# A two-layer hybrid decoder trunk: another order of TensorE's work at the block boundaries

## The chip, the cores and the metric

The kernel runs on one core of a Trainium2 chip. The metric is device time in microseconds (us) for one execution; one execution is also taken by the hardware profiler, and its span and its rows are quoted here. TensorE (PE in the profile) multiplies and transposes, VectorE (DVE) and ScalarE (ACT) do the elementwise work, GpSimd (POOL) takes square roots of reciprocals as powers and starts the DMAs that add onto a tile, and SyncE (SP) starts the plain loads.

## The reference

Each of two layers updates 512 tokens of 1024 features three times. With `h = rmsnorm(x)`:

```python
x = x + 0.5 * swiglu(rmsnorm(x, ffn1_norm), w1, w3, w2)     # d_ff 2816
p = rmsnorm(x, mix_norm) @ w_in                             # 8 pieces of 256 columns
mix = concat([conformer_conv(...), short_gated_conv(...), multiscale_pool(...), chunked_spatial_gating(...)])
x = x + mix @ w_out
x = x + 0.5 * swiglu(rmsnorm(x, ffn2_norm), w1, w3, w2)
```

After the second layer one more rmsnorm gives the output. All values are float32.

## The kernel before

**Tokens and numbers.** The 512 tokens stand in four blocks `b` of 128 rows; the "later" tokens are blocks 2 and 3 (half `r = 1`), the earlier ones blocks 0 and 1 (half `r = 0`). The residual stream lies in SBUF as `xt[b]`, token rows by features. Every float32 matrix is split into a high part (rounded to the matmul type by ScalarE) and a low part (the rest, subtracted by VectorE), and each product is three matmuls, high by high, weight-high by low (or the reverse), and low by high: `mm3`, whose three matmuls are lines 107, 108 and 109 of the profile. So every matrix on either side costs a cast on ScalarE and a subtraction on VectorE before all its three matmuls can run.

**A boundary.** At the end of a block (feed-forward or mixers) the result of each token block is added to `xt[b]` by VectorE. `Norm.square` (line 136, ScalarE) sums the squares of half a row, and `Norm.scale` (line 141) adds them up (`nv`, line 147), takes the power on POOL (`ry`, line 114) and makes the normed rows `xn` on VectorE (line 150), in one of two buffers. `Norm.turn(b)` (line 169) turns `xn` with 8 transposes on TensorE (line 157) and splits the result into high (line 204 or 183, ScalarE) and low parts (line 205 or 184, VectorE). The next block's matmuls read those splits: `B12` and `B22` for the later tokens, `B11` and `B21` for the earlier ones in a feed-forward, `h` and `l` in the mixers. The feed-forwards use one level of a Strassen-like scheme over halves of the tokens, and so also sums of these operands (`T1` to `T4`, `third` and `split`).

**Names.** `f0a`, `f0b`, `f1a`, `f1b` are the four feed-forwards in order, `L0` and `L1` the mixers of the two layers: f0a, L0, f0b, f1a, L1, f1b. Norm `n` feeds f0a, `m` feeds the mixers, `b` feeds f0b and f1b, and `a` feeds f1a.

**The start of a feed-forward (`up`).** It begins with the odd last slice of the hidden units: 4 weight tiles `w[m, k]` (two for each half `m` of that slice) are cast and split (`whi`, line 272; `wlo`, line 274), then for `r` = 1 and 0, for `m`, for `e` (w1 or w3) and for eight steps `k`, `mm3` follows. That is 96 matmuls of 256 columns for each `r`. Between the two `r` stand `third()` and `turns()`, the 16 transposes of the earlier token blocks. After it the ten other slices go through seven products each; slice 0 has two DMAs on POOL that add one weight tile onto another (lines 327 and 330), each after the plain load of the tile underneath.

**The end of the mixers.** `part(b, c)` (line 749) is 18 matmuls of 512 columns for one token block and one half of the features. After the last of these parts, an ending of 6 matmuls for each `b` and `c` adds the conformer's share, in the order `b` = 2, 3, 0, 1; then both blocks of the later tokens are turned. The weights of the endings (`wa`) lie in four tiles at `q0` to `q3`; `q2` and `q3` are also the home of `B22` and `B12`. The three `whi` and `wlo` buffers are shared: the next feed-forward's first splits take those that the last `part` has read.

**The start of the mixers.** `values(1)`, then the gate and the value projection of the later tokens, `turns()`, then both projections of the earlier tokens.

**What sets the order.** TensorE's instructions go out as they stand in the program (`tc.manual_schedule` at the bottom), and it works them off in that order. In `down`, VectorE and ScalarE also have the written order. Everywhere else a scheduler at build time orders each engine's queue by priority and by when it thinks the operands are there; `tc.high_priority` lifts the boundary's steps. Each engine then works its queue in order.

Of the kernel before, what the change touches and what calls it, by code (L numbers as in the profile page):

```python
# [10 lines left out]
F32 = mybir.dt.float32  # L11
F32R = mybir.dt.float32r
AF = mybir.ActivationFunctionType
ALU = mybir.AluOpType

P = 128
T = 512
D = 1024
KD = D // P
# [30 lines left out]
def trunk(ctx: ExitStack, tc: tile.TileContext, x, par, gains, tab, w13, w2, wi, wg, wo, out):  # L50
    nc = tc.nc
    V, S, G, PE = nc.vector, nc.scalar, nc.gpsimd, nc.tensor

    const = ctx.enter_context(tc.tile_pool(name="const", bufs=1))
    acts = ctx.enter_context(tc.tile_pool(name="acts", bufs=1))
# [15 lines left out]
    xt = [acts.tile([P, D], F32, name=f"x{b}", tag=f"x{b}") for b in range(NB)]  # L71
# [13 lines left out]
    def bank(name, shape=(P, T)):  # L85
        return psm.tile(list(shape), F32, tag="ps", name=name)


    def load(src, shape, name):
        raw = wts.tile(list(shape), F32, tag="raw", name=f"raw_{name}", bufs=6)  # L90
        nc.sync.dma_start(raw, src)
        return raw

    def split_w(raw, shape, name, pool=None, tags=("whi", "wlo")):
        pool = pool or wts
        hi = pool.tile(list(shape), F32R, tag=tags[0], name=f"whi_{name}")
        S.copy(hi, raw)  # L97
        lo = pool.tile(list(shape), F32R, tag=tags[1], name=f"wlo_{name}")
        V.tensor_tensor(lo, raw, hi.bitcast(F32), ALU.subtract)
        return hi, lo  # L100
# [4 lines left out]
    def mm3(ps, sh, sl, mh, ml, first, last, more=False):  # L105

        PE.matmul(ps, sh, mh, start=first, stop=False, skip_group_check=more)  # L107
        PE.matmul(ps, sh, ml, start=False, stop=False, skip_group_check=more)  # L108
        PE.matmul(ps, sl, mh, start=False, stop=last, skip_group_check=more)  # L109
# [128 lines left out]
    HALF = (slice(0, 256), slice(256, 512))  # L238
# [3 lines left out]
    def up(f, nrm, turns, name):  # L242
# [18 lines left out]
        def quarters(i):  # L261
            return {
                (m, k): load(w13[f, i, m, k], W, f"{name}{i}{m}{k}") for m in range(2) for k in range(2)
            }
# [3 lines left out]
        raw = quarters(i)  # L268
        w = {}
        for n, (m, k) in enumerate(((0, 0), (0, 1), (1, 0), (1, 1))):  # L270
            hi = wts.tile(list(W), F32R, tag="whi" if n < 3 else "raw", name=f"whi_{name}{i}{m}{k}", bufs=3 if n < 3 else 6)
            S.copy(hi, raw[m, k])
            lo = wts.tile(list(W), F32R, tag="wlo" if n < 3 else "raw", name=f"wlo_{name}{i}{m}{k}", bufs=3 if n < 3 else 6)
            V.tensor_tensor(lo, raw[m, k], hi.bitcast(F32), ALU.subtract)
            w[m, k] = hi, lo
        ps = {(m, e): bank(f"p{2 * e + 1}_{name}{i}{m}") for m in range(2) for e in range(2)}
        for r in (1, 0):
            for m in range(2):
                for e in range(2):
                    for k in range(KD):  # L280
                        hi, lo = w[m, k // 4]
                        g = nrm.op[f"B{k // 4 + 1}{r + 1}"]
                        mm3(
                            ps[m, e][:, HALF[r]], hi[:, e, k % 4], lo[:, e, k % 4],
                            g[0][:, k % 4], g[1][:, k % 4], k == 0, k == KD - 1,
                        )
            if r == 1:
                nrm.third()
                turns()
        for m in range(2):  # L290
            sg = tmp.tile([P, T], F32, tag="sg", name=f"sg_{name}{i}{m}", bufs=1)
            S.activation(sg, ps[m, 0], AF.Silu)
# [23 lines left out]
        for i in range(KH - 1):  # L316
            j, jj = i // 2, i % 2
            to = {(m, r): a[m][j][:, jj, HALF[r]] for m in range(2) for r in range(2)}
            nm = f"{name}{i}"
# [215 lines left out]
    def ffn(f, nrm, nxt, name, turns, end=False):  # L535
        down(f, *up(f, nrm, turns, name), nxt, name, end)
# [23 lines left out]
    def mixers(l, nrm, nxt, turns):  # L560
        base = l * C_LAYER
        nm = f"L{l}"
        scratch = Scratch(nm)

        def col(c):
            return pt[:, c : c + 1]
# [14 lines left out]
        def proj_mm(p, w, c=slice(0, T)):  # L581
            for k in range(KD):
                ks = slice(k * P, (k + 1) * P)
                mm3(p[:, c], w[0][:, ks], w[1][:, ks], nrm.h(k)[:, c], nrm.l(k)[:, c], k == 0, k == KD - 1)
# [9 lines left out]
        for i, home in enumerate(((acts, ("a04", "a14")), (None, ("whi", "wlo")))):  # L594
            raw = load(wg[l, :, i * D : (i + 1) * D], (P, D), f"{nm}g{i}")
# [42 lines left out]
        wgate, wval = proj_w(2), proj_w(0)  # L638
        pg, pv = bank(f"pi_{nm}2"), bank(f"pi_{nm}0")
        proj_mm(pg, wgate, HALF[1])  # L640
        proj_mm(pv, wval, HALF[1])
        turns()
        proj_mm(pg, wgate, HALF[0])
        proj_mm(pv, wval, HALF[0])
        gated(0, pg, pv)
# [4 lines left out]
        mix = {}  # L650
# [90 lines left out]
        wr, pw = {}, {}  # L741
# [7 lines left out]
        def part(b, c):  # L749
            pw[b, c] = bank(f"po_{nm}{b}{c}")  # L750
            bs = slice(b * P, (b + 1) * P)
            for i in range(3):
                for e in range(2):
                    hi, lo = mix[MIX_ORDER[2 * i + e]]
                    mm3(
                        pw[b, c], hi[:, bs], lo[:, bs], wr[c, i][0][:, e], wr[c, i][1][:, e],
                        i == 0 and e == 0, False,
                    )
# [25 lines left out]
        for b in range(NB):  # L784
            for j in range(2):
                PE.matmul(
                    pst[:, b : b + 1], ya[j][0][:, b * P : (b + 1) * P], ones[:, 0:1],
                    start=(j == 0), stop=(j == 1),
# [10 lines left out]
        for j in range(2):  # L799
            y, sg = ya[j][1], ya[j][0]  # L800
            g, b = col(base + C_CG + j), col(base + C_CBB + j)
# [4 lines left out]
            mix[j] = split2(y, f"ya_{nm}{j}")  # L806


        wa = []
        for c in range(2):  # L810
            raw = load(wo[l, c, :, 6:8], (P, 2, T), f"{nm}oa{c}")
            wa.append(split_w(raw, (P, 2, T), f"{nm}oa{c}", acts, (f"q{2 * c}", f"q{2 * c + 1}")))
        part(0, 1)
        part(1, 1)
        for b in (2, 3, 0, 1):
            bs = slice(b * P, (b + 1) * P)
            for c in range(2):
                for e in range(2):
                    hi, lo = mix[e]
                    mm3(pw[b, c], hi[:, bs], lo[:, bs], wa[c][0][:, e], wa[c][1][:, e], False, e == 1)  # L820
                with tc.high_priority(offset=400):
                    xs = xt[b][:, c * T : (c + 1) * T]
                    V.tensor_tensor(xs, pw[b, c], xs, ALU.add)
                nxt.square(b, c)
            nxt.scale(b)
        for b in (2, 3):
            nxt.turn(b)


    ctx.enter_context(tc.manual_schedule(engines={mybir.EngineType.PE}))  # L830
# [4 lines left out]
    nrm = Norm("n0", 0)  # L835
# [14 lines left out]
    for l in range(DEPTH):  # L850

        def turns(nrm=nrm):
            for b in (0, 1):
                nrm.turn(b)

        nx = Norm(f"m{l}", 3 * l + 1)
        ffn(2 * l, nrm, nx, f"f{l}a", turns)
        nrm = nx

        def turns(nrm=nrm):  # L860
            for b in (0, 1):
                nrm.turn(b)

        nx = Norm(f"b{l}", 3 * l + 2)
        mixers(l, nrm, nx, turns)
        nrm = nx

        def turns(nrm=nrm):
            for b in (0, 1):
                nrm.turn(b)  # L870

        nx = Norm(f"a{l + 1}", 3 * l + 3)
        ffn(2 * l + 1, nrm, nx, f"f{l}b", turns, end=l + 1 == DEPTH)
        nrm = nx
# [84 lines left out]
```

## Time and profile before

| | |
|---|---|
| median of 3 runs | 1709.82 us (1709.77 to 2012.91) |
| profiled execution, its own time | 1710.36 us |
| its span, first to last instruction | 1708.7 us |
| TensorE busy | 1661.4 us, 97% of the span, 11072 matmuls and transposes |
| VectorE, ScalarE, GpSimd busy | 77%, 50%, 8% |

The profiled execution's own time stands 0.54 us above the median, and 1.7 us of it lie outside the span. Times in rows are us from the span's start.

### The profile page before, as it was taken

To read this page: it belongs to the slowest core of one execution; us is meant where nothing else is said; L and a number is where in the kernel's file an instruction comes from. 1 tells how busy PE (TensorE), PEld (TensorE's weight loads), DVE (VectorE), ACT (ScalarE), POOL (GpSimd) and SP (SyncE) were. 2 spreads that over 40 slices of the span, in tenths; PEclk is the share of its full clock that TensorE was granted. 3 is DMA by queue.
4 is the path that set the end of the run, shared out by engine and by line. 5 is a ranking of instruction groups with operands and counts; after the bars stand their busy time and mean duration, and the time that the engine had idled before them with its cause. 6 is when DMAs were issued, how large, how long until landed. Compare 5 with 4: busy or idle time off the path is not lost.

```text
span 1708.7 us, 27504 instructions
## 1 busy us (share of the span) xinstructions
PE 1661.4 (97%) x11072; PEld 1517.7 (89%) x11072; DVE 1310.9 (77%) x1661; ACT 850.0 (50%) x1238; POOL 140.2 (8%) x170
## 2 busy tenths in 40 slices
PE   8999999989999999999999999999999999999997
PEld 8999998778779999988699999886887799999875
DVE  5777778879856777788887777888796577777986
ACT  5454555553344554556554554555433455545554
POOL 1000002010010001001000000010000101000100
PEclk9999999999999999999999999999999999999999
DMA  6776669543332777769457777694323346776872
GB/s 199 190 181 173 174 173 263 179 154 100 111 86 71 183 194 185 183 191 258 131 137 182 191 183 190 186 258 160 124 89 97 87 122 183 181 186 181 228 220 82
DMA packets 80479, 283.94 MB, mean 166 GB/s; under 512 B 8928, under 2 KB 9056, under 8 KB 80352
## 3 DMA queue, kind: packets, MB, share of 16 engines
q1 hardware_dynamic: 61920, 217.18, 38.7%
q0 software_dynamic: 18432, 65.02, 21.9%
q8 instruction: 86, 1.41, 0.3%
q14 instruction: 41, 0.34, 0.1%
HBM read 280.07 MB, written 2.10 MB: 165 GB/s over the span
## 4 chain that ended last, share of the span: by engine, by line
PE 83%; DVE 10%; issue 3%; ACT 3%; DMA 1%; POOL 0%; POOLq 0%; ACTq 0%; DVEq 0%; SPq 0%
PE pi_L L108 3%; PE pi_L L107 3%; PE pi_L L109 3%; PE px_f1b L109 3%; PE px_f1a L109 3%; PE px_f0a L109 3%; PE px_f1b L107 3%; PE px_f1a L107 3%; PE px_f0a L107 3%; PE px_f0a L108 3%; PE px_f1b L108 3%; PE px_f1a L108 3%; PE px_f0b L109 3%; PE px_f0b L107 3%; PE px_f0b L108 3%
## 5 line engine op out<-in xcount | busy, mean ns | idle before, releaser
L107 PE MATMUL pi_L<-gh_m,whi_L1i 128*128 128x512 f32 (+1 forms) x128 | 47.5, 371 | 0.3 <-ACT gh_m L183 0.3
L107 PE MATMUL pi_L<-gh_m,whi_L0i 128*128 128x512 f32 (+1 forms) x128 | 47.5, 371 | 0.3 <-ACT gh_m L183 0.3
L108 PE MATMUL pi_L<-gl_m,whi_L0i 128*128 128x512 f32 (+1 forms) x128 | 46.6, 364 | 0.6 <-DVE gl_m L184 0.6
L108 PE MATMUL pi_L<-gl_m,whi_L1i 128*128 128x512 f32 (+1 forms) x128 | 46.6, 364 | 0.6 <-DVE gl_m L184 0.6
L109 PE MATMUL pi_L<-gh_m,wlo_L1i 128*128 128x512 f32 (+1 forms) x128 | 46.4, 363 | 0.0
L109 PE MATMUL pi_L<-gh_m,wlo_L0i 128*128 128x512 f32 (+1 forms) x128 | 46.4, 363 | 0.0
L770 DVE SCALAR_TENSOR_TENSOR scr_gv_L<-scr_cv_L,pt,scr_gv_L 128x511 f32<-128x511 f32 (+29 forms) x60 | 43.8, 731 | 0.6
L770 DVE SCALAR_TENSOR_TENSOR scr_cv_L<-scr_cv_L,pt,scr_cv_L 128x511 f32<-128x511 f32 (+29 forms) x60 | 43.7, 728 | 0.1
L107 PEld LDWEIGHTS pi_L<-gh_m,whi_L0i 128*128 128x128 f32 x128 | 24.2, 189 | 4.9 <-ACT gh_m L183 0.6
L108 PEld LDWEIGHTS pi_L<-gl_m,whi_L1i 128*128 128x128 f32 x128 | 24.2, 189 | 4.8 <-DVE gl_m L184 0.8
L108 PEld LDWEIGHTS pi_L<-gl_m,whi_L0i 128*128 128x128 f32 x128 | 24.2, 189 | 4.8 <-DVE gl_m L184 0.8
L107 PEld LDWEIGHTS pi_L<-gh_m,whi_L1i 128*128 128x128 f32 x128 | 24.2, 189 | 4.8 <-ACT gh_m L183 0.6
L97 ACT CAST whi_L1i<-raw_L1i 128x1024 fp32r<-128x1024 f32 x14 | 14.6, 1050 | 27.3 <-PE pi_L L108 16.4
L97 ACT CAST whi_L0i<-raw_L0i 128x1024 fp32r<-128x1024 f32 x14 | 14.6, 1049 | 27.3 <-PE pi_L L108 16.4
L109 PEld LDWEIGHTS pi_L<-gh_m,wlo_L1i 128*128 128x128 f32 x128 | 24.2, 189 | 3.8
L109 PEld LDWEIGHTS pi_L<-gh_m,wlo_L0i 128*128 128x128 f32 x128 | 24.2, 189 | 3.8
L136 ACT ACTIVATE sq_a<-x 128x512 f32<-128x512 f32 x16 | 10.1, 632 | 29.3 <-DVE x L475 29.2
L205 DVE TENSOR_TENSOR B_b<-pt_b,B_b 128x512 fp32r<-128x512 f32 x16 | 10.1, 681 | 18.5 <-ACT B_b L204 18.5
L108 PE MATMUL p_f0b<-B_b,whi_f0b 128*128 128x256 f32 x64 | 19.4, 303 | 2.9 <-DVE B_b L205 2.9
L136 ACT ACTIVATE sq_m<-x 128x512 f32<-128x512 f32 x16 | 10.1, 632 | 24.0 <-DVE x L475 23.9
L108 PE MATMUL p_f1b<-B_b,whi_f1b 128*128 128x256 f32 x64 | 19.0, 298 | 2.8 <-DVE B_b L205 2.8
L107 PE MATMUL p_f0b<-B_b,whi_f0b 128*128 128x256 f32 x64 | 19.2, 300 | 2.5 <-ACT B_b L204 2.5
(3183 smaller groups left out, 7303.2 us busy)
## 6 DMA issues: line engine op xcount, KB each, us to landing
raw_L0i<-wi SPq DMA_DIRECT2D x14, 512.0 KB, 3.7
raw_L1i<-wi SPq DMA_DIRECT2D x14, 512.0 KB, 3.7
tt_f0a<-w POOLq DMA_DIRECT2D x10, 512.0 KB, 7.2
tt_f0b<-w POOLq DMA_DIRECT2D x10, 512.0 KB, 7.8
tt_f1a<-w POOLq DMA_DIRECT2D x10, 512.0 KB, 7.6
tt_f1b<-w POOLq DMA_DIRECT2D x10, 512.0 KB, 8.4
gain<-gains SPq DMA_DIRECT2D x7, 512.0 KB, 4.1
raw_L0o<-wo SPq DMA_DIRECT2D x6, 512.0 KB, 3.9
```

The source lines that it names most:

```text
L97: S.copy(hi, raw)
L107: PE.matmul(ps, sh, mh, start=first, stop=False, skip_group_check=more)
L108: PE.matmul(ps, sh, ml, start=False, stop=False, skip_group_check=more)
L109: PE.matmul(ps, sl, mh, start=False, stop=last, skip_group_check=more)
L136: S.activation(sq, xt[b][:, c * T : (c + 1) * T], AF.Square, scale=1.0 / 32.0, accum_out=self.ss[b][:, c : c + 1],)
L205: V.tensor_tensor(lo[:, :, s], ps[q], hi[:, :, s].bitcast(F32), ALU.subtract)
L770: V.scalar_tensor_tensor(acc[:, kk:], v[:, : T - kk], cw, acc[:, kk:], ALU.mult, ALU.add)
```

## The change

Four places in the order of TensorE's program are written anew; no matmul, transpose, cast or subtraction is added or dropped.

- `up`: `third()` is called ahead of the matmuls. For each `r` and `m`, all 16 high-by-high matmuls (over `e` and `k`) come first, then the 16 that need the operand's low part, then the 16 that need the weight's low part. `turns()` stands after the first 64 of the 96 matmuls of `r` = 1, so 32 of them follow it.
- `mixers`, start: `turns()` moves between the gate and the value projection of the later tokens.
- `mixers`, end: the endings of blocks 2 and 3 come before `part(1, 1)`, and the turn of block 2 stands inside block 0's ending, that of block 3 inside block 1's.
- The endings' weights lie in two tiles at `q0` and `q1`, which leaves `q2` and `q3` free.

```diff
--- before.py
+++ after.py
@@ -274,19 +274,20 @@
             V.tensor_tensor(lo, raw[m, k], hi.bitcast(F32), ALU.subtract)
             w[m, k] = hi, lo
         ps = {(m, e): bank(f"p{2 * e + 1}_{name}{i}{m}") for m in range(2) for e in range(2)}
+        nrm.third()
+
         for r in (1, 0):
             for m in range(2):
-                for e in range(2):
-                    for k in range(KD):
-                        hi, lo = w[m, k // 4]
-                        g = nrm.op[f"B{k // 4 + 1}{r + 1}"]
-                        mm3(
-                            ps[m, e][:, HALF[r]], hi[:, e, k % 4], lo[:, e, k % 4],
-                            g[0][:, k % 4], g[1][:, k % 4], k == 0, k == KD - 1,
-                        )
-            if r == 1:
-                nrm.third()
-                turns()
+                for n, (x, y) in enumerate(((0, 0), (0, 1), (1, 0))):
+                    if (r, m, n) == (1, 1, 1):
+                        turns()
+                    for e in range(2):
+                        for k in range(KD):
+                            PE.matmul(
+                                ps[m, e][:, HALF[r]], w[m, k // 4][x][:, e, k % 4],
+                                nrm.op[f"B{k // 4 + 1}{r + 1}"][y][:, k % 4],
+                                start=n == 0 and k == 0, stop=n == 2 and k == KD - 1,
+                            )
         for m in range(2):
             sg = tmp.tile([P, T], F32, tag="sg", name=f"sg_{name}{i}{m}", bufs=1)
             S.activation(sg, ps[m, 0], AF.Silu)
@@ -638,8 +639,8 @@
         wgate, wval = proj_w(2), proj_w(0)
         pg, pv = bank(f"pi_{nm}2"), bank(f"pi_{nm}0")
         proj_mm(pg, wgate, HALF[1])
+        turns()
         proj_mm(pv, wval, HALF[1])
-        turns()
         proj_mm(pg, wgate, HALF[0])
         proj_mm(pv, wval, HALF[0])
         gated(0, pg, pv)
@@ -806,25 +807,34 @@
             mix[j] = split2(y, f"ya_{nm}{j}")
 
 
-        wa = []
+
+        wah, wal = (acts.tile([P, 2, 2, T], F32R, tag=f"q{e}", name=f"oa{'hl'[e]}_{nm}") for e in range(2))
         for c in range(2):
             raw = load(wo[l, c, :, 6:8], (P, 2, T), f"{nm}oa{c}")
-            wa.append(split_w(raw, (P, 2, T), f"{nm}oa{c}", acts, (f"q{2 * c}", f"q{2 * c + 1}")))
+            S.copy(wah[:, c], raw)
+            V.tensor_tensor(wal[:, c], raw, wah[:, c].bitcast(F32), ALU.subtract)
+
+        def ending(b, c):
+            bs = slice(b * P, (b + 1) * P)
+            for e in range(2):
+                hi, lo = mix[e]
+                mm3(pw[b, c], hi[:, bs], lo[:, bs], wah[:, c, e], wal[:, c, e], False, e == 1)
+            with tc.high_priority(offset=400):
+                xs = xt[b][:, c * T : (c + 1) * T]
+                V.tensor_tensor(xs, pw[b, c], xs, ALU.add)
+            nxt.square(b, c)
+
         part(0, 1)
+        for b in (2, 3):
+            ending(b, 0)
+            ending(b, 1)
+            nxt.scale(b)
         part(1, 1)
-        for b in (2, 3, 0, 1):
-            bs = slice(b * P, (b + 1) * P)
-            for c in range(2):
-                for e in range(2):
-                    hi, lo = mix[e]
-                    mm3(pw[b, c], hi[:, bs], lo[:, bs], wa[c][0][:, e], wa[c][1][:, e], False, e == 1)
-                with tc.high_priority(offset=400):
-                    xs = xt[b][:, c * T : (c + 1) * T]
-                    V.tensor_tensor(xs, pw[b, c], xs, ALU.add)
-                nxt.square(b, c)
+        for b in (0, 1):
+            ending(b, 0)
+            nxt.turn(2 + b)
+            ending(b, 1)
             nxt.scale(b)
-        for b in (2, 3):
-            nxt.turn(b)
 
 
     ctx.enter_context(tc.manual_schedule(engines={mybir.EngineType.PE}))
```

## Rows read from the trace of the kernel before

**Rows 1.** The page: busy time of each engine, its share and its instructions.
```profile
PE 1661.4 (97%) x11072; PEld 1517.7 (89%) x11072; DVE 1310.9 (77%) x1661; ACT 850.0 (50%) x1238; POOL 140.2 (8%) x170
```

**Rows 2.** Stretches: length, busy us of PE, PEld, DVE, ACT, POOL, granted clock, DMA.
```profile
36.00:244.00 208.00, 208.00 (x1736) 208.00 (x1735) 154.29 (x183) 105.82 (x145) 15.71 (x18) 1.00 0.67 176
513.68:520.50 6.82, 4.91 (x23) 4.91 (x24) 5.06 (x6) 3.44 (x6) 0.00 (x0) 0.50 0.28 78
18.74:22.15 3.41, 2.92 (x13) 2.92 (x14) 3.41 (x4) 1.71 (x3) 0.00 (x0) 0.50 0.47 151
528.00:533.00 5.00, 4.10 (x33) 3.66 (x32) 2.50 (x5) 2.05 (x4) 0.00 (x0) 1.00 0.00 0
1356.80:1360.20 3.40, 3.40 (x17) 3.40 (x17) 2.15 (x3) 2.09 (x4) 0.00 (x0) 0.50 0.43 154
```

**Rows 3.** Timeline of TensorE, start of f0b: start, us, instruction, idle before it.
```profile
508.88 1.91 PE L157 MATMUL pt_b<-ident,xn_b 128*128 128x128 f32 x16
512.91 0.38 PE L107 MATMUL p_f0b<-B_b,whi_f0b 128*128 128x256 f32 x1 [2.13 <-ACT B_b L204]
515.59 0.58 PE L108 MATMUL p_f0b<-B_b,whi_f0b 128*128 128x256 f32 x1 [2.30 <-DVE B_b L205]
...
532.44 0.39 PE L108 MATMUL p_f0b<-B_b,whi_f0b 128*128 128x256 f32 x1 [0.56 <-DVE B_b L205]
```

**Rows 4.** Timeline of TensorE, start of f1b.
```profile
1350.15 1.91 PE L157 MATMUL pt_b<-ident,xn_b 128*128 128x128 f32 x16
...
1372.78 0.39 PE L108 MATMUL p_f1b<-B_b,whi_f1b 128*128 128x256 f32 x1 [0.56 <-DVE B_b L205]
```

**Rows 5.** Timeline of ScalarE, TensorE and VectorE, start of f0a.
```profile
14.59 2.02 ACT L272 CAST whi_f0a<-raw_f0a 128x1024 fp32r<-128x1024 f32 x2
...
15.72 0.39 PE L107 MATMUL p_f0a<-B_n,whi_f0a 128*128 128x256 f32 x1 [1.77 <-ACT whi_f0a L272]
...
17.96 2.35 DVE L274 TENSOR_TENSOR wlo_f0a<-raw_f0a,whi_f0a 128x1024 fp32r<-128x1024 f32 x2
...
35.09 0.39 PE L108 MATMUL p_f0a<-B_n,whi_f0a 128*128 128x256 f32 x1 [0.56 <-DVE B_n L205]
```

**Rows 6.** Timeline of TensorE, end of f0b and start of f1a.
```profile
854.08 1.91 PE L157 MATMUL pt_a<-ident,xn_a 128*128 128x128 f32 x16
855.74 0.48 PE L107 MATMUL pz_f0b<-whi_f0bg,as_f0bg 128*128 128x512 f32 x1
...
859.92 0.28 PE L107 MATMUL p_f1a<-B_a,whi_f1a 128*128 128x256 f32 x1
...
876.00 0.39 PE L108 MATMUL p_f1a<-B_a,whi_f1a 128*128 128x256 f32 x1 [0.56 <-DVE B_a L205]
```

**Rows 7.** Timeline of VectorE and GpSimd, start of f1a.
```profile
866.44 1.29 DVE L150 SCALAR_TENSOR_TENSOR xn_a<-x,ry_a,gain 128x1024 f32<-128x1024 f32 x1 [1.22 <-POOL ry_a L114]
...
870.15 0.89 POOL L330 DMA_DIRECT2D raw_f1a0e<-w  x1 [3.75 <-DVE nv_a L147]
...
871.67 1.28 DVE L150 SCALAR_TENSOR_TENSOR xn_a<-x,ry_a,gain 128x1024 f32<-128x1024 f32 x1 [2.09 <-POOL ry_a L114]
```

**Rows 8.** Timeline of VectorE and TensorE, start of the mixers L0.
```profile
370.24 1.28 DVE L150 SCALAR_TENSOR_TENSOR xn_m<-x,ry_m,gain 128x1024 f32<-128x1024 f32 x1 [0.44 <-POOL ry_m L114]
...
375.54 1.91 PE L157 MATMUL pt_m<-ident,xn_m 128*128 128x128 f32 x16
...
378.74 0.38 PE L108 MATMUL pi_L<-gl_m,whi_L0i 128*128 128x256 f32 x1 [0.56 <-DVE gl_m L184]
```

**Rows 9.** Timeline of four engines, end of the mixers L0.
```profile
495.47 1.05 ACT L272 CAST whi_f0b<-raw_f0b 128x1024 fp32r<-128x1024 f32 x1 [4.86 <-PE po_L L109]
...
500.49 0.39 PE L109 MATMUL po_L<-whi_L0oa,scr_ya_L01h 128*128 128x512 f32 x1
...
503.84 1.28 DVE L150 SCALAR_TENSOR_TENSOR xn_b<-x,ry_b,gain 128x1024 f32<-128x1024 f32 x1 [0.76 <-POOL ry_b L114]
...
506.32 0.89 POOL L330 DMA_DIRECT2D raw_f0b0e<-w  x1 [2.51 <-DMA raw_f0b0e<-w]
```

## Prediction

> **What bounds the kernel now.** I read the page first. TensorE is busy 97% of the span [rows 1], so no other engine's time counts unless TensorE stands still for it, and the change takes no matmul away. What it can give back is TensorE's idle time and time at the lower clock. For these I read TensorE's own list of waits and then its timeline, boundary by boundary, beside the views of stretches that give the granted clock. The reader is to see three things. In the middle of a feed-forward TensorE starts a 256-column matmul every 0.120 us (208.00 us for 1736) with no idle time [rows 2]; that is the price of steady work. At the start of f0b it stands 2.13 us and then 2.30 us with one matmul between, because the casts and subtractions that follow the turn have nothing in front of them [rows 3]. And the granted clock then falls to 0.50, 1.2 instead of 2.4 GHz, for 6.82 us [rows 2], where 256 columns cost double.
>
> **The change part by part.** The measure for each boundary is the stretch from a fixed point to the start of the steady `r` = 0 matmuls, now and in the new order. Sixteen transposes among other matmuls cost 1.66 us, from 854.08 to 855.74 [rows 6]; so 32 cost 3.32 us and 8 cost 0.83 us. The 96 matmuls of `r` = 1 cost 96 x 0.120 = 11.5 us.
>
> *Mixers into f0b and f1b.* Now: from the first transpose, 508.88, to 532.32 (one matmul ahead of the second `r` = 0 matmul, 532.44) is 23.44 us [rows 3]; for f1b 1350.15 to 1372.66, 22.51 us [rows 4]. New: 3.32 + 11.5 = 14.8 us if nothing waits, a gain of 8.6 and 7.7 us. It consists of the two idle times, the half clock (0.50 over 6.82 and 3.40 us [rows 2]), and the waits after the second set of transposes.
>
> Does anything wait? I set up TensorE's new clock. A 512-column matmul starts every 0.227 us (37 between 500.49 [rows 9] and 508.88 [rows 3]), so a part of 18 takes 4.1 us, an ending of six 1.36 us. The endings of blocks 2 and 3 start where `part(1, 1)` stood, 4.1 us earlier than 497.99, and end at 496.6 and 499.4. Block 2's normed rows now end at 505.12, 4.4 us after its last matmul's time is up at 500.72 [rows 9]; in the new order that is about 501.0, and block 3's 503.8. The turns are due at 504.8 and 508.3: 3.8 and 4.5 us of slack. This slack is work that stands in between: `part(1, 1)` and block 0's and 1's endings. Without it the cost is the 2.13 + 2.30 us of now. The feed-forward starts at 510.5. The last cast of block 3's high parts may be 0.3 us late, and the low parts have 1.9 us of high-by-high matmuls as cover. I take 0.5 us for what remains (bounds 0 and 3, the latter if squares, sums and splits queue behind each other on ScalarE and VectorE): 8.1 and 7.2 us.
>
> What moves with it: the next feed-forward's splits wait for buffers that `part(1, 1)` reads (the cast at 495.47 was released by TensorE [rows 9]). That part now runs 24 matmuls later, so these splits do too, by 5.4 us, to about 501 to 506. They still end before 510.5, so they cost nothing on TensorE, but they sit among the boundary's steps on VectorE. SyncE's loads for slice 0 and the POOL DMAs behind them also move by 5.4 us, the second from 506.32 [rows 9] to about 511.8; the products that need them come after the `r` = 0 matmuls, more than 10 us later. The powers stand in the same POOL queue, which is the second and third rival.
>
> Block 1's rows are turned after 64 matmuls and 8 transposes, 510.5 + 7.7 + 0.8 = 519.0; they should be there 4.4 to 5.7 us after the last ending, by 516.2. So nothing is lost there.
>
> *f0a.* Now 15.72 to 34.97, 19.25 us [rows 5]. New: 11.5 + 1.66 = 13.2 us, plus a wait: the second weight cast ends at 16.61, while four matmuls from 15.72 use up only 0.5 us, so 0.5 us. The two weight low parts that the third group needs end at 20.3 [rows 5], in time for its second half at 20.5. Gain 5.6 us. Of that, 1.7 us rests on the clock not falling again (3.41 us at 0.50, [rows 2]); without it 3.9 us.
>
> *f1a.* This boundary has no endings to hide things, and here the new order loses. Now 859.92 to 875.88, 15.96 us [rows 6]. New: `turns()` is due after 64 matmuls, at 867.6. Block 0's rows are there (866.44 + 1.29 = 867.7). Block 1's are not: they end at 872.96, as the power for them stands on POOL behind an adding DMA at 870.15, and the sum before it stood behind block 0's rows on VectorE, whose order in `down` is fixed [rows 7]. Nothing in that chain reads what the new order brings forward. So TensorE stands at the second half of the transposes from 868.4 to 872.96, 4.5 us, with the 32 remaining matmuls queued behind: 872.96 + 0.83 + 3.83 = 877.6, 1.7 us later than now. What used to hide the late rows was the 32 matmuls that now follow the turn. Such an idle stretch (4.5 us, transposes on either side) is the nearest thing to f0b's 2.13 and 2.30, after which the clock fell, so I add one stretch at half clock, as long as the shortest in the rows: half of 3.4 us, 1.7 us [rows 2]. Loss 3.4 us (bounds: a gain of 2.8 if the rows come in time, 15.96 - 13.2; a loss of 5.5 if the earlier casts delay them by two more).
>
> In the Trainium skill (TensorE: Matmul & The Clock Gate, PE-mode transpose) it says that transposes do not count as busy for the clock in the way matmuls do. Here 16 transposes and the waits behind them left the clock at 1.00, with matmuls on both sides, in the stretch from 528 on [rows 2]. By that rule f1a's two sets of transposes would belong to the idle stretch and a fall would be sure; by that row alone it would not come, and the sum would be 1.7 us lower.
>
> *Start of the mixers (two).* Now 375.54 to 378.62, 3.08 us; new 1.66 us, since 24 matmuls (2.9 us) stand between the transposes and their reader: a gain of 1.4 us. The turn is due at 372.7; block 1's rows are there at 371.5 [rows 8]. With 0.1 us kept back for ScalarE's other work there, 1.3 us each, 2.6 us.
>
> *At no cost.* `third()` is called earlier, but its subtraction and split go to VectorE and ScalarE, where they stand behind the same work as before, and their reader is a product after the `r` = 0 matmuls. The endings' weights need as many casts as before; two tiles instead of four leave `q2` and `q3` for `B22` and `B12`, without which the turns inside the endings would wait for the last ending. Grouping the matmuls by part changes which weights follow each other, but each matmul has its own weight load now (11072 of both [rows 1]).
>
> *Sum:* 8.1 + 7.2 + 5.6 - 3.4 + 2.6 = 20.1 us. From the profiled execution's own 1710.36 that is 1690.3, and by the 0.54 us by which it exceeds the median, 1689.8: forecast 1690 us.
>
> **The rivals.**
> *f1a is not late.* If the scheduler puts the power ahead of the adding DMA, the rows come in time: 1690 - 3.4 - 2.8 = 1683.8 us. For it: nothing ties the two. Against: none of their operands moves, so their order has no reason to.
> *The late rows come at f0b and f1b too.* The POOL DMA moved to 511.8 stands just where block 0's power is due (510), and VectorE has the moved splits to do. If block 1's rows came as late as in f1a, each boundary would pay f1a's 4.5 + 1.7 us: 1690 + 12.4 = 1702 us. Against: 2.8 us of slack.
> *The clock still falls at three starts* (f0a, f0b, f1b), 1.7 us each: 1695 us. The Trainium skill's sentence on transposes, told above, speaks for it: eight stand inside an ending of both earlier blocks. By the rows, f0a's fall at 18.74 came after 1.66 us of transposes and a stand-still with three matmuls, and the new order fills only the latter.
> *Slower: both adding DMAs ahead of block 2's power.* If POOL's queue has them first, the power waits for the load under the second DMA, due at 511.8. By the 2.8 us from that DMA to the end of the rows (870.15 to 872.96, [rows 7]) block 2 is ready at 514.6, and TensorE stands at the first turn from 504.8, 9.8 us, with all endings and the feed-forward behind it, and loses the clock (1.7 to 2.5 us). Twice: 1690 + 24 = 1714 us. It decides from 10 us lost per boundary. For it: this queue held one of the DMAs ahead of each of the two powers before. Against: the powers now come earlier and the DMAs later.
> *The change does not take effect:* ScalarE and VectorE get another queue order and the readers wait as before: 1710 us.
>
> **How the numbers follow.** Forecast 0.58; f1a in time 0.12; late rows at f0b and f1b 0.14; clock 0.10; slower 0.03; no effect 0.03. The range 1682 to 1703 takes in the forecast with its bounds, the first three rivals' middles, and leaves out some 0.1 to 0.2. Two per cent is about what a measurement of this kernel can tell from no change, 34 us; below 1675.6 there is nothing in the cases but their errors (all gains at their best bounds give 1682), 0.03; above 1744 even less, 0.02; within, 0.95.
>
> **What would show it.** In the new profile: no idle time over 1 us on TensorE between the endings and slice 0 of f0b and f1b, and a granted clock of 1.00 there; transposes of f0b at about 504.8 and 508.3 by this clock; no wait at the `r` = 0 matmuls; at f1a one idle stretch of some 4.5 us ahead of the transposes of block 1, ended by `xn_a`. It is wrong if TensorE waits inside the endings for `xn_b`, if f1a has no stand-still, or if stretches at half clock turn up elsewhere.

## The result, and the profile after

The changed kernel takes 1693.12 us (median of 4 runs, 1692.39 to 1693.51), the kernel before in the same comparison 1710.67 us: a ratio of 0.9893, 95% interval 0.9879 to 0.9907, so 1.1% faster, clear of the noise. The profiled execution took 1693.16 us with a span of 1691.5 us, 17.2 us less than the 1708.7 us of before. (One of the four runs of before was a slow one, 2012.91 us; the ratio leaves it out, but the 1710.67 us is the median of all four.)

The page, first part, of the changed kernel: the same work in less time [rows 1].

```profile
PE 1656.6 (98%) x11072; PEld 1515.8 (90%) x11072; DVE 1311.9 (78%) x1661; ACT 850.2 (50%) x1238; POOL 139.4 (8%) x170
```

Where did 17.2 us come from? Both traces have the same landmarks, so the difference between them can be read place by place. Starts are us from each span's start.

| landmark | before | after | difference | since the landmark above | predicted |
|---|---|---|---|---|---|
| f0a, first matmul | 15.72 | 16.51 | +0.79 | +0.79 | 0 |
| f0a, first product of slice 0 | 46.59 | 41.85 | -4.74 | -5.53 | -5.6 |
| mixers L0, first matmul | 364.03 | 359.74 | -4.29 | +0.45 | 0 |
| L0, first matmul with `w_out` | 459.74 | 454.17 | -5.57 | -1.28 | -1.3 |
| f0b, first product of slice 0 | 543.92 | 530.94 | -12.98 | -7.41 | -8.1 |
| f1a, first matmul | 859.92 | 846.68 | -13.24 | -0.26 | 0 |
| f1a, first product of slice 0 | 887.50 | 877.93 | -9.57 | +3.67 | +3.4 |
| mixers L1, first matmul | 1205.27 | 1195.89 | -9.38 | +0.19 | 0 |
| L1, first matmul with `w_out` | 1300.98 | 1290.36 | -10.62 | -1.24 | -1.3 |
| f1b, first product of slice 0 | 1384.27 | 1367.12 | -17.15 | -6.53 | -7.2 |
| end | 1708.66 | 1691.46 | -17.20 | -0.05 | 0 |

The change takes effect at six places, gains at five and loses at one, f1a. The timeline of TensorE in the changed kernel, end of L0 and start of f0b, answers to [rows 3] (line 286 is the feed-forward's new matmul; here and below the last row of a view can be cut off by its end):

```profile
499.23 1.04 PE L157 MATMUL pt_b<-ident,xn_b 128*128 128x128 f32 x8
...
502.86 1.03 PE L157 MATMUL pt_b<-ident,xn_b 128*128 128x128 f32 x8
...
505.11 2.91 PE L286 MATMUL p_f0b<-B_b,whi_f0b 128*128 128x256 f32 x20
...
508.48 1.69 PE L286 MATMUL p_f0b<-B_b,whi_f0b 128*128 128x256 f32 x12 [0.46 <-DVE B_b L205]
510.01 2.08 PE L286 MATMUL p_f0b<-B_b,wlo_f0b 128*128 128x256 f32 x16
...
519.42 1.24 PE L286 MATMUL p_f0b<-B_b,whi_f0b 128*128 128x256 f32 x9
```

The two turns stand inside the endings and wait for nothing; the first matmul follows the last ending; of the 2.13 and 2.30 us of idle time one of 0.46 us is left (and one of 0.10 us ahead of it); the second set of transposes has 32 matmuls behind it and no wait. The start of f1a in the same view answers to [rows 6]:

```profile
846.68 4.24 PE L286 MATMUL p_f1a<-B_a,whi_f1a 128*128 128x256 f32 x32
850.75 2.08 PE L286 MATMUL p_f1a<-B_a,wlo_f1a 128*128 128x256 f32 x16
852.67 2.08 PE L286 MATMUL p_f1a<-B_a,whi_f1a 128*128 128x256 f32 x16
854.59 1.06 PE L157 MATMUL pt_a<-ident,xn_a 128*128 128x128 f32 x8
860.08 1.97 PE L157 MATMUL pt_a<-ident,xn_a 128*128 128x128 f32 x8 [4.42 <-DVE xn_a L150]
861.70 2.95 PE L286 MATMUL p_f1a<-B_a,whi_f1a 128*128 128x256 f32 x16
864.49 2.08 PE L286 MATMUL p_f1a<-B_a,wlo_f1a 128*128 128x256 f32 x16
866.41 1.84 PE L286 MATMUL p_f1a<-B_a,whi_f1a 128*128 128x256 f32 x14
```

Here TensorE stands 4.42 us between the transposes of block 0 and those of block 1, released by `xn_a`. The 8 transposes that follow take 1.62 us to the next row instead of 0.8, and the next 16 matmuls 2.79 instead of 1.92 us. The view of stretches says why (columns as in [rows 2]):

```profile
497.00:526.00 29.00, 28.44 (x212) 26.80 (x211) 24.93 (x33) 18.27 (x30) 3.53 (x5) 1.00 0.43 109
348.08:351.49 3.41, 3.41 (x10) 2.62 (x9) 3.01 (x4) 0.69 (x2) 0.26 (x1) 0.50 0.42 139
860.08:863.49 3.41, 3.41 (x16) 3.41 (x17) 2.62 (x5) 1.17 (x2) 0.00 (x0) 0.50 0.97 264
1184.35:1187.76 3.41, 3.41 (x10) 2.65 (x9) 2.92 (x4) 0.85 (x3) 0.35 (x1) 0.50 0.50 153
```

The start of f0b now keeps 1.00; after the stand-still of f1a comes a stretch at 0.50, 1.2 GHz. The stretch at 1184 has its like in the trace of before (at 1192.92), the one at 348, just ahead of L0, has not.

### The profile page after: what moved, and what is told of

It reads as the page before. It is cut to its first block, busy times and chain, and to the rows that moved or that the text cites. A ratio compares the mean times of both kernels' runs of the same rounds, so it can differ in the third digit from the quotient of the medians.

```text
span 1691.5 us, 27502 instructions
## 1 busy us (share of the span) xinstructions
PE 1656.6 (98%) x11072; PEld 1515.8 (90%) x11072; DVE 1311.9 (78%) x1661; ACT 850.2 (50%) x1238; POOL 139.4 (8%) x170
## 4 chain that ended last, share of the span: by engine, by line
PE 84%; DVE 9%; ACT 3%; issue 3%; DMA 1%; POOL 0%; POOLq 0%; ACTq 0%; DVEq 0%
PE pi_L L107 3%; PE pi_L L108 3%; PE pi_L L109 3%; PE px_f1a L109 3%; PE px_f0b L109 3%; PE px_f0a L109 3%; PE px_f1b L109 3%; PE px_f0a L107 3%; PE px_f1b L108 3%; PE px_f0b L108 3%; PE px_f1a L107 3%; PE px_f0a L108 3%; PE px_f1b L107 3%; PE px_f0b L107 3%; PE px_f1a L108 3%
## 5 line engine op out<-in xcount | busy, mean ns | idle before, releaser
L99 DVE TENSOR_TENSOR wlo_L1i<-raw_L1i,whi_L1i 128x1024 fp32r<-128x1024 f32 x14 | 17.0, 1218 | 3.8 <-ACT whi_L1i L97 3.8
L99 DVE TENSOR_TENSOR wlo_L0i<-raw_L0i,whi_L0i 128x1024 fp32r<-128x1024 f32 x14 | 17.0, 1214 | 3.8 <-ACT whi_L0i L97 3.8
L824 DVE TENSOR_TENSOR x<-po_L,x 128x512 f32<-128x512 f32 x16 | 11.0, 685 | 11.0 <-PE po_L L109 11.0
L286 PE MATMUL p_f0a<-B_n,whi_f0a 128*128 128x256 f32 x128 | 16.6, 285 | 2.0 <-ACT whi_f0a L272 2.0
```

The costliest lines, as they stand in the source:

```text
L286: PE.matmul(ps[m, e][:, HALF[r]], w[m, k // 4][x][:, e, k % 4], nrm.op[f"B{k // 4 + 1}{r + 1}"][y][:, k % 4], start=n == 0 and k == 0, sto ...
```

## The experiments

The theory: each boundary pays for itself, by the idle time that the new order covers, and f1a loses, because the turn comes before the rows of block 1 are ready. "The start" of a feed-forward is below the time from its first matmul to its first `r` = 0 matmul: in the changed kernel 13.82 us at f0a, 14.31 at f0b and f1b, 19.73 at f1a.

**One part alone: the feed-forward's start (e1) and the end of the mixers (e2).** The kernel before, with the first of the four edits, or with the endings' order and the two tiles.

> The kernel before with the new order of the feed-forward's start alone (grouping by part, turn of the earlier tokens after 64 matmuls); both ends of the mixers as before. Theory (each boundary pays for itself, f1a loses): f0a about 5.5 us shorter, f1a about 3.7 us longer with one stand-still of 4.4 us for block 1's normed rows, f0b and f1b 2 to 3 us shorter each, since casts still follow the turn with nothing in front of them but the low parts get 16 matmuls of cover: about 1703 us. Rival (the grouping does all the work at f0b and f1b): these two 7 us shorter each, about 1694 us. Rival (the new order of the ends matters alone): no shorter than before, 1710 us.

> The kernel before with the new end of the mixers alone. Theory: the feed-forwards f0b and f1b start right after the last ending, wait 1 to 2.5 us for the low parts of the operand (which come second in the old order of each group of three) and pay 1.4 us after the second turn, so 4 to 6 us shorter each; the clock stays at 1.00 there; f0a and f1a as before: about 1700 us. Rival (the grouping does all the work): 1710 us, with TensorE waiting at the start of f0b as long as before.

e1 took 1700.33 us (ratio 0.9938, 0.9923 to 0.9953), e2 1702.65 us (0.9955, 0.994 to 0.997). At f0b the first part gained 5.0 us and the second 4.9 from the first `w_out` matmul to the first product, and both together 7.4; at f1b it was 3.4, 4.0 and 6.5. They cover in part the same waits, so the sum of the two would be too much. The timeline of TensorE at f0b in e1 shows what the grouping does by itself:

```profile
503.43 1.91 PE L157 MATMUL pt_b<-ident,xn_b 128*128 128x128 f32 x16
507.18 0.74 PE L286 MATMUL p_f0b<-B_b,whi_f0b 128*128 128x256 f32 x4 [1.84 <-ACT B_b L204]
508.15 2.45 PE L286 MATMUL p_f0b<-B_b,whi_f0b 128*128 128x256 f32 x16 [0.23 <-ACT B_b L204]
511.05 1.70 PE L286 MATMUL p_f0b<-B_b,whi_f0b 128*128 128x256 f32 x12 [0.46 <-DVE B_b L205]
```

The first wait, for the casts, stays (1.84 us); the second, for the low parts, shrinks from 2.30 to 0.46 us. e1 had f1a's stand-still too (3.55 us), e2 had not, and f1a's start was there as long as before. That places the loss in the moved turn or the grouping, not in the mixers' new end. At f0b and f1b e1 gained more than the 2 to 3 us expected, and e2's 4.9 and 4.0 us lie in the expected 4 to 6, with a wait of 1.89 us left for the low parts. In e2's trace f0a, which that edit does not touch, took 1.4 us longer than before, with 6.83 us at half clock instead of 3.41.

The moved turn at the start of the mixers was not run alone. But e1 and e2 lack it, and from the first matmul of L0 to the first with `w_out` they take 95.71 and 95.70 us, as before (95.71); so the 1.28 and 1.24 us in the table come with that edit.

**The moved turn of f1a put back (e4).**

```diff
-                    if (r, m, n) == (1, 1, 1):
+                    if (r, m, n) == ((0, 0, 0) if name == "f1a" else (1, 1, 1)):
                         turns()
```

> The changed kernel with the turn of the earlier tokens of f1a alone back behind all 96 matmuls of the later tokens. Theory (the moved turn is what loses there): f1a's start takes 15.5 us instead of 19.7 us (rows of block 1 13.3 us after the first matmul, then 0.8 us of transposes and 1.4 us of waiting for their splits), about 1689 us. Rival (f1a loses for another reason, the grouping or the clock): within 1 us of the changed kernel.

1688.19 us (0.9869, 0.9854 to 0.9884). f1a's start took 14.84 us, 4.9 less than in the changed kernel, and the clock stayed up there. With 96 matmuls first, the wait for block 1's rows is 0.71 us. The rival falls: the loss is the place of the turn. (The intervals of the two ratios just touch, at 0.9884 and 0.9879, but the four runs, 1688.05 to 1688.44 us, lie well below the changed kernel's.)

**Why are the rows late? The sums first (e3), and then the powers ahead of the DMAs (e5).** In `down`, VectorE works in the written order. e3 changes it for the last step; e5 also has slice 0 load the two tiles for the adding DMAs last, which puts both powers of f1a ahead of both DMAs on POOL.

```diff
                 if end:
                     nxt.last(t)
-                else:
-                    nxt.scale(t)
+                elif t == 1:
+                    nxt.scale(0)
+                    nxt.scale(1)
```

> The changed kernel, and in the feed-forward's last step VectorE adds block 1's result and ScalarE squares it before block 0's rows are normed (in the fixed order of these two engines); no instruction more or less. Theory (f1a's stand-still is the fixed order on VectorE, which puts block 1's sum behind block 0's rows, and the POOL queue): block 1's rows come about 4 us earlier, the stand-still shrinks from 4.4 us to under 1.5 us and the clock stays at 1.00 at f1a: 5 to 6 us less than the changed kernel, about 1687.5 us. Rival (the stand-still is the adding DMA on POOL alone): 1 us less at most. Rival (something on TensorE's side, a bank or its own queue, holds the second turn): no difference, 1693 us.

> The kernel with the sums first (block 1's sum ahead of block 0's rows), and slice 0's two loads that the adding DMAs need come last of its five loads, which puts both powers of f1a ahead of both adding DMAs in POOL's queue. Theory (what is left of f1a's stand-still, 1.8 us, is the power of block 0 behind the first adding DMA): block 1's rows 1.2 to 1.5 us earlier, stand-still under 0.6 us, about 1687.3 us. Rival (ScalarE and VectorE, busy with splits, hold the rows): the stand-still stays at 1.5 to 1.8 us, 1688.7 us.

e3 took 1688.72 us (0.9869, 0.9853 to 0.9886). TensorE's wait for `xn_a` fell from 4.42 to 1.82 us and the clock stayed up; f1a's start took 15.57 us. POOL in e3:

```profile
851.61 0.89 POOL L328 DMA_DIRECT2D raw_f1a0d<-w  x1 [12.48 <-DVE wlo_f1a L274]
852.22 0.86 POOL L114 TENSOR_TENSOR ry_a<-nv_a,expo 128x1 f32<-128x1 f32 x1
854.67 1.40 POOL L114 TENSOR_TENSOR ry_a<-nv_a,expo 128x1 f32<-128x1 f32 x1 [1.59 <-DVE nv_a L147]
857.90 0.89 POOL L331 DMA_DIRECT2D raw_f1a0e<-w  x1 [1.83 <-DMA raw_f1a0e<-w]
```

In this queue the second power stands ahead of the second DMA; the edit broke both links, the late sum and the DMA ahead of the power, at once. The rows of block 1 tell the two apart, first in the changed kernel, then in e3:

```profile
856.10 0.21 DVE L147 TENSOR_SCALAR nv_a<-ss_a 128x1 f32<-128x1 f32 x1
857.23 0.89 POOL L331 DMA_DIRECT2D raw_f1a0e<-w  x1 [4.10 <-DVE B_a L205]
857.84 0.86 POOL L114 TENSOR_TENSOR ry_a<-nv_a,expo 128x1 f32<-128x1 f32 x1
858.74 1.29 DVE L150 SCALAR_TENSOR_TENSOR xn_a<-x,ry_a,gain 128x1024 f32<-128x1024 f32 x1 [1.68 <-POOL ry_a L114]
```

```profile
854.32 0.21 DVE L147 TENSOR_SCALAR nv_a<-ss_a 128x1 f32<-128x1 f32 x1
856.10 1.28 DVE L150 SCALAR_TENSOR_TENSOR xn_a<-x,ry_a,gain 128x1024 f32<-128x1024 f32 x1 [0.44 <-POOL ry_a L114]
```

f1a's first matmul is at 846.68 in the one and at 846.63 in the other, so the rows start 2.6 us earlier in e3: 1.7 us because the sum of squares (`nv_a`) is there earlier, and 0.9 us because the way from it through POOL to the rows takes 1.78 instead of 2.64 us. What is left is block 0's power behind the first DMA. e5 takes that away too: the wait was 0.51 us and f1a's start 14.24 us, as the theory says. But e5 took 1689.49 us (0.988, 0.9865 to 0.9894), no less than e3. Its own list of TensorE's waits shows where the 1.3 us went:

```profile
PE px_f0b L107 <- ACT sn_f0b L354: 0.8, 1, 0.8
...
PE px_f0a L107 <- ACT sn_f0a L354: 0.6, 1, 0.6
```

At f0b the copy that TensorE waits for stands on ScalarE behind a cast, and that cast waits for a tile that a late DMA adds to:

```profile
541.57 1.05 ACT L97 CAST whi_f0b0e<-raw_f0b0e 128x1024 fp32r<-128x1024 f32 x1 [5.16 <-DMA raw_f0b0e<-w]
...
543.78 0.57 ACT L354 COPY sn_f0b<-px_f0b 128x512 f32<-128x512 f32 x1
```

From slice 0's first product to the next landmark f0a and f0b each take 0.9 us longer than in e3. The DMAs on POOL were early for a reason.

**The four tiles again (e6).** `wah` and `wal` replaced by the four tiles at `q0` to `q3`.

> The changed kernel with the endings' weights in four tiles at q0 to q3, as before. Theory (q2 and q3 had to be freed for the early turns to be of use): the casts of the later tokens' operands wait for the last ending, TensorE stands 1.5 to 3 us at the start of f0b and f1b, perhaps with the clock falling (1.7 us each): 1696 to 1701 us. Rival (the tiles don't matter): 1693 us.

1697.15 us (0.9921, 0.9906 to 0.9935). The timeline of TensorE at f0b: the turns are where they were, and the first matmuls wait for the casts, which a matmul of the last ending released (ScalarE's row is the last).

```profile
499.24 1.03 PE L157 MATMUL pt_b<-ident,xn_b 128*128 128x128 f32 x8
502.87 1.03 PE L157 MATMUL pt_b<-ident,xn_b 128*128 128x128 f32 x8
506.70 0.74 PE L286 MATMUL p_f0b<-B_b,whi_f0b 128*128 128x256 f32 x4 [1.43 <-ACT B_b L204]
508.32 1.93 PE L286 MATMUL p_f0b<-B_b,whi_f0b 128*128 128x256 f32 x14 [0.89 <-ACT B_b L204]
```

```profile
505.09 1.56 ACT L204 CAST B_b<-pt_b 128x512 fp32r<-128x512 f32 x3 [0.23 <-PE po_L L108]
```

So the early turns are worth 1.8 us less at each of the two boundaries when the home of their splits is still read by the last ending.

**The old grouping (e10).** Inside `r` and `m`, for each `e` and `k` the three matmuls of `mm3`, as before.

> The changed kernel with the old order inside the feed-forward's start, three matmuls for each k (high by high, high by low, low by high); the turn of the earlier tokens stands after 63 matmuls. Theory (the grouping hides the low parts behind 16 high-by-high matmuls): f0a's start 3 to 5 us longer than the changed kernel's 13.8 us, f0b's and f1b's 1.5 to 2 us longer each than 14.3 us, f1a's hidden in its stand-still: 1699 to 1702 us. Rival (the place of the turns does it all): within 1 us of 1693 us.

1701.1 us (0.9945, 0.993 to 0.996). f0a's start took 19.31 us (13.82 in the changed kernel), f0b's 16.89 and f1b's 15.39 (14.31), f1a's 19.48 (19.73, hidden in the stand-still, as expected). At f0b the second matmul waited 1.90 us for the low part, and a stretch at half clock followed:

```profile
509.57 0.28 PE L107 MATMUL p_f0b<-B_b,whi_f0b 128*128 128x256 f32 x1
511.75 0.39 PE L108 MATMUL p_f0b<-B_b,whi_f0b 128*128 128x256 f32 x1 [1.90 <-DVE B_b L205]
```

At f0a the old order brought back the clock's fall (6.83 us at 0.50 from 18.28 on; 28 matmuls lie 0.213 us apart there and 0.118 us after it, so the clock's share of the 5.5 us is 2.7). At f1b the wait for the low part was as long as at f0b, 1.90 us, and no stretch at half clock followed. The grouping is worth 8.0 us (1701.1 less 1693.12) of the 17.2; by the starts it is 5.5 at f0a, 2.6 at f0b and 1.1 at f1b, and e10's first matmul came 1.0 us earlier than the changed kernel's, which is not its doing.

**What lets the clock fall at f1a? The stand-still filled with matmuls (e7) or with transposes (e8).**

```diff
+            if self.name == "a1" and (b, q) == (1, 0):
+                for _ in range(18):                                        # e7
+                    PE.matmul(ps[:, 0], mean_w, mean_w, start=True, stop=True)
+                for _ in range(36):                                        # e8 instead
+                    PE.transpose(ps[:, 0], self.xn[0][:, 0:P], ident)
             for k in range(4):
                 c = (4 * q + k) * P
```

> The changed kernel, and in f1a's stand-still, between the transposes of block 0 and of block 1, 18 extra 128-column float32 matmuls (36 instructions, 3.9 us) into the bank that the transposes then fill; nothing reads them. Theory (the fall of the clock at 860 us follows the stand-still and costs 1.7 us of its own): the clock stays at 1.00 at f1a and the start of r = 0 comes 1.6 us earlier after f1a's first matmul, 18.1 instead of 19.7 us; in all 1691.5 us. Rival (the clock falls by itself, whatever TensorE does there): 19.7 us, 1693 us.

> The same with 36 extra transposes of block 0's rows in place of the extra matmuls (about as long, 3.8 us); nothing reads them. Theory (transposes keep the clock up as matmuls do): as with the extra matmuls, 18.1 us, 1691.5 us. Rival (the rule of the Trainium skill, TensorE: Matmul & The Clock Gate, PE-mode transpose: transposes don't count as busy): the clock falls at f1a all the same, 19.7 us, 1693 us.

e7 took 1690.73 us (0.9885, 0.9871 to 0.99), e8 1691.03 us (0.9886, 0.9869 to 0.9902); f1a's start took 17.53 and 18.45 us. One row of the view of stretches, 846 to 866, of the changed kernel, of e7 and of e8:

```profile
846.00:866.00 20.00, 15.58 (x113) 15.01 (x112) 16.28 (x23) 8.93 (x15) 2.96 (x4) 0.91 0.74 185
```

```profile
846.00:866.00 20.00, 20.00 (x168) 19.68 (x167) 17.64 (x24) 9.88 (x16) 2.96 (x4) 1.00 0.72 185
```

```profile
846.00:866.00 20.00, 19.20 (x163) 18.76 (x162) 16.62 (x23) 9.01 (x16) 2.96 (x4) 1.00 0.71 183
```

The granted clock stands after the five busy times: 0.91 with the stand-still, 1.00 with useless matmuls in it, and 1.00 with transposes. TensorE in e8, where 44 transposes run from 853.89 to 858.85 with no matmul among them:

```profile
853.89 1.04 PE L160 MATMUL pt_a<-ident,xn_a 128*128 128x128 f32 x8
854.76 4.09 PE L157 MATMUL pt_a<-ident,xn_a 128*128 128x128 f32 x36
859.66 1.09 PE L160 MATMUL pt_a<-ident,xn_a 128*128 128x128 f32 x8 [0.80 <-DVE xn_a L150]
```

So the fall at f1a follows from TensorE's standing still, and transposes kept the clock as matmuls did. The other traces agree: the four with a stand-still of 3.18 us or more at f1a (4.42 us in the changed kernel, 3.55 in e1, 3.58 in e6, 3.18 in e10) all have a stretch at half clock there, the eight with waits of 1.82 us or less have none. The Trainium skill (TensorE: Matmul & The Clock Gate, PE-mode transpose) has it that transposes do not count as busy in the same way; the measurement of e8 says otherwise for these float32 ones, and decides. From the first transpose of block 1 to the first `r` = 0 matmul the changed kernel takes 6.33 us, e7 4.71 and e8 4.75, so the half clock costs 1.6 us. The rest of the difference at f1a, 2.2 us in e7 and 1.3 in e8, is that block 1's transposes began 12.82 and 13.70 us after the first matmul instead of 13.40. The medians, 2.4 and 2.1 us below the changed kernel's, agree, but the intervals of the ratios overlap with its own, so this reading rests on the traces.

**Both together (e9).** The sums first, and in all feed-forwards the turn after 80 matmuls, `(1, 1, 2)` in place of `(1, 1, 1)`.

> The kernel with the sums first, and in all four feed-forwards the turn of the earlier tokens after 80 instead of 64 matmuls. Theory (a turn pays if it stands after the rows are ready and with at least the splits' 1.4 us of matmuls behind it): at f1a the due time moves from 8.5 to 10.4 us after the first matmul, the stand-still of 1.8 us shrinks to under 0.4 us, the 16 matmuls that remain (1.9 us) hide the splits, the start takes 13.6 us instead of 15.6 us; the three others are unchanged: 1686.7 us. Rival (16 matmuls are too few to hide the splits): up to 1 us more at each of the four starts, 1688 to 1691 us.

1686.38 us, with 1686.02 to 1689.16 over four runs; ratio 0.9858, 0.9841 to 0.9874, the fastest of all. f1a's start took 13.83 us; the timeline of TensorE there, in e9:

```profile
854.62 4.00 PE L286 MATMUL p_f1a<-B_a,whi_f1a 128*128 128x256 f32 x32
858.46 2.25 PE L157 MATMUL pt_a<-ident,xn_a 128*128 128x128 f32 x16
860.47 2.15 PE L286 MATMUL p_f1a<-B_a,wlo_f1a 128*128 128x256 f32 x16
862.45 2.80 PE L286 MATMUL p_f1a<-B_a,whi_f1a 128*128 128x256 f32 x22
```

The 16 transposes run as one group (0.12 us of waiting inside), and the 16 matmuls behind them hide the splits. The starts of f0b and f1b are as in the changed kernel, 14.33 and 14.32 us. The profiled execution, 1689.16 us, was the longest of the four; its clock fell once at f0a (3.41 us from 17.36), which put that start at 15.19 instead of 13.82 us, after the same waits (1.77 and 0.22 us) as in the eight other traces with the new start of f0a, in none of which it fell there. Against e3 and e4, the intervals of the ratios overlap; the traces alone tell them apart, by 1.7 and 1.0 us at f1a.

## Why the prediction was right, point by point

The forecast was 1690 us; the measurement is 3.1 us above, within the range. The two per cent that the prediction took for what a measurement can tell from no change was far too wide: the interval of the ratio is 0.28% wide.

*Mixers into f0b and f1b.* The mechanism was as told: turns inside the endings, no wait, the clock kept, and the second set of transposes hidden. By the old clock (5.57 us had been gained by then) the turns of f0b stand at 504.8 and 508.4, as foretold. The gains of 8.1 and 7.2 us were 7.4 and 6.5: I had taken 0.5 us for what remains, and it is 1.2 us (bounds 0 and 3). Most of it lies around the two waits for the low parts, 0.56 us together: the first 20 matmuls take 3.37 us, 0.97 more than at 0.120 each. e6 and e10 show that the two edits given as "at no cost" and as cover are needed: without the free tiles 1.8 us are lost at each boundary, without the grouping the low parts are waited for.

*f0a.* Gain 5.6, measured 5.5. The clock did not fall again, which I had put at 1.7 us of it. e10 shows that it fell when the low parts were waited for, but e9 shows that the new start does not rule it out: it fell in one of the nine traces with that start, and in all three with the old one (before, e2, e10). So this part of the gain was likely, not certain. (When the clock fell at 18.74 in the kernel before, two matmuls, not three, had run between the waits.)

*Start of the mixers.* 1.3 us each, measured 1.28 and 1.24.

*f1a.* The loss was 3.4 us, measured 3.7; the stand-still 4.5, measured 4.42; and the half clock after it came, 3.41 us long, at a price of 1.6 us by e7 and e8 against the 1.7 in the sum. ("256 columns cost double" was a little too much: at half clock they took 0.213 us in e10, 1.8 times the 0.120.) e4 shows that it is the moved turn, e3 and e5 that the late rows are the fixed order on VectorE and the powers behind POOL's DMAs. That nothing in this chain would move held: the rows of block 1 end 13.0 us after f1a's first matmul before [rows 6, 7], and 13.4 us after it now.

*The rivals.* POOL's queue decides the first, the second and the fourth of them, not the third. "f1a is not late" did not happen, since POOL's queue kept its order. "Late rows at f0b and f1b too" came nearer than I thought. The second DMA was to come at 511.8; it came at 510.58, which is 516.2 by the old clock, and so just ahead of block 1's power; POOL and VectorE of the changed kernel:

```profile
510.58 0.90 POOL L331 DMA_DIRECT2D raw_f0b0e<-w  x1 [5.27 <-DVE T3f_b L219]
511.19 0.87 POOL L114 TENSOR_TENSOR ry_b<-nv_b,expo 128x1 f32<-128x1 f32 x1
```

```profile
512.10 1.28 DVE L150 SCALAR_TENSOR_TENSOR xn_b<-x,ry_b,gain 128x1024 f32<-128x1024 f32 x1 [1.72 <-POOL ry_b L114]
```

The rows end at 513.4 and block 1's transposes begin at about 514.7, so the slack is 1.3 us, not 2.8. "Slower" did not happen: the powers of blocks 2 and 3 (493.58 and 497.93) now stand ahead of both DMAs.

*What I had not in the sum.* 0.8 us at the very start: the 80 warm-up matmuls took longer (11.86 against 11.07 us in the rows of line 844 and, before, 834), ahead of anything that changed. Over the twelve traces f0a's first matmul comes at 15.39 to 16.69 us, so this is not the change. And 0.45 us up to the start of L0, where the clock now fell and before did not. By the prediction's own words a stretch at half clock elsewhere is a sign of being wrong, and this is one. But e2, whose source is that of before up to the end of the mixers, has it as well (3.41 us from 352.75), so it comes without the change too; of the twelve traces only before and e10 lack it, and why stays open.

## What to carry to other kernels

Where one engine is busy 97% of the time, what is to be had is at the boundaries, and each is worth what its waits and the half clock after them cost: put independent matmuls between a transpose and its reader, and start with the products that need only the operand that is ready first. But a step that is moved ahead on an in-order engine must find its input there: compute the due time and the ready time at every boundary where it occurs, for at the one where the input came late the same edit lost 3.7 us. And free the home of an early result, or part of its early start is lost (1.8 us at each boundary here).

## What the runs showed of the hardware

Transposes kept TensorE's clock at 2.4 GHz as matmuls did (granted 1.00 over 20 us, with 44 transposes in a row and 0.80 us of waiting behind them), while a stand-still of 4.42 us with transposes on either side was followed by 3.41 us at 1.2 GHz. At that clock 8 transposes took 1.62 us.

The length of a single wait did not settle whether the clock fell. One of 1.90 us at f0b was followed by a stretch at 1.2 GHz, one as long at f1b of the same trace (e10) was not, nor were the two of 1.89 us in e2 or the one of 1.82 us in e3. And after the same waits at f0a (1.77, 0.80 and 1.94 us) the stretch was 3.41 us long in the kernel before and 6.83 us in e2 and e10.
